# A third seven-product pair in the down projections, and the mixer's transposes' transfers issued from SyncE

## The chip, the cores and the metric

The kernel runs on one core of one Trainium2 chip. The time is device microseconds of one execution of the whole layer, from the first to the last instruction with what lies around them. The core's engines are TensorE (PE, with its weight loads as PEld), VectorE (DVE), ScalarE (ACT), GpSimd (POOL) and SyncE (SP); each runs its own list of instructions in order and waits on semaphores. DMA engines move data between HBM and the on-chip SBUF, on request of SP, POOL or ACT.

## The reference

One decoder layer in float32: 256 positions, model width 2048, inner width 5632. Cut to what matters:

```
def swiglu(h, w_gate, w_up, w_down):
    return (jax.nn.silu(h @ w_gate) * (h @ w_up)) @ w_down

x = x + 0.5 * swiglu(rms_norm(x, ffn1_norm), ffn1_w_gate, ffn1_w_up, ffn1_w_down)
h = rms_norm(x, mix_norm);  proj = h @ w_in
# q, k: per-head norm and rotary; dilated and differential attention -> o_dil, o_diff
y = sigmoid(g_dil) * (o_dil @ w_dil_branch) + sigmoid(g_diff) * (o_diff @ w_diff_branch)
x = x + y @ w_out
x = x + 0.5 * swiglu(rms_norm(x, ffn2_norm), ffn2_w_gate, ffn2_w_up, ffn2_w_down)
```

The middle part, between the two SwiGLU blocks, is called the mixer here.

## The kernel before

**Products.** Every float32 factor is split in two float32r parts, a high one (a rounded copy made by ACT) and a low one (the rest, a subtraction on DVE), and one product of blocks is three matmuls (`three`, L147 to L152): high x high, high x low, low x high. Each matmul takes 128 rows of the contraction, 128 positions and 512 columns of a weight. The activations stand in SBUF with the contraction on the partitions, 16 k tiles of 128 (20 or 24 for the down products), already split (`xh`, `xl`; `ah`, `al` for the down products).

**Weights.** They stream from HBM in pieces of 2 k tiles x 512 columns (512 KB), each into a tile `raw`, requested by SP. ACT and DVE split a piece into `w_hi` and `w_lo` (`parts`, L106, its instructions at L110 and L111; in `linear` L125 and L126). There are five pairs of split tiles, and four `raw` tiles, six inside the two SwiGLU blocks. A piece can be requested when a `raw` tile is free, that is when DVE has split what was in it, and it can be split when PE has used up an older split tile. So SP, ACT, DVE and PE form a chain of buffers that lets the splits run some pieces ahead of PE.

**Seven products for eight.** `two_chunks` (L176) computes two 512-column chunks at once. A pair of k tiles, u, is then a 2 x 2 block product (2 k tiles, 2 halves of the positions, 2 column chunks), which costs 8 block products, 24 matmuls. For the pairs named in `WINO` (gate and up) and `WINO_DOWN` (down), it takes seven block products, 21 matmuls, by sums of blocks (Winograd's form of Strassen's method). The sums of the x blocks are made once for all column chunks (`sums_of_x`, L154): per pair an addition, four small sums, a split, in a `raw` tile f that is held meanwhile. The sums of the weight blocks are made anew in each call: after the first split of the pair's two pieces, four subtractions on DVE overwrite the raw pieces (L217 to L220, L218 and after wait for each other), and then ACT and DVE split them a second time. So an ordinary pair needs two splits of 128x1024, and a seven-product pair three and a half and the four subtractions. After the last such pair ACT and DVE add up the partial results (L230 to L234), and at the end of a call DVE adds them to the others (L236).

**A SwiGLU block** (`ffn`, L361). Eleven chunks of 512 inner columns are done in two halves of 6 and 5 (`HALVES`). In a half, each chunk's gate and up columns are one call of `two_chunks` (the very first chunk is two calls of `linear`); DVE multiplies (L387), turns the result on 32x32 blocks (L279), and two DMAs through HBM finish the transpose (`turn_blocks`, L273, issued from POOL: `blocks<-turned`, then `moved<-blocks` once the first has landed). A deferred `split_blocks` then writes `ah`, `al`. At the end of a half the sums of x for the down products are made, and the down products follow: two calls of `two_chunks` in the first half, one and two `linear` in the second. So there are six such calls in the kernel's two blocks, and four "half starts", where the down products begin right behind the last gate and up chunk. On DVE the end of that chunk (L231 to L236, L387, L279) stands between the splits for the down products.

**The mixer** also uses `turn_blocks`, for the queries and keys (`qk_chunk`, L560), for y and for the residual. POOL runs its DMA requests and the powers for the norms (L246) in one list.

**Order.** The order on each engine is made when the kernel is built, by a scheduler that takes the program in the order written and moves instructions by its own estimate of when they can start.

Of the kernel before, what the change touches and what calls it, by code (L numbers as in the profile page):

```python
# [11 lines left out]
F32 = mybir.dt.float32  # L12
F32R = mybir.dt.float32r
I32 = mybir.dt.int32
AF = mybir.ActivationFunctionType
ALU = mybir.AluOpType
# [3 lines left out]
P = 128  # L20
# [14 lines left out]
WINO = (3, 5)  # L35
WINO_DOWN = (3, 6)
HALVES = (6, 5)
# [18 lines left out]
def hybrid_layer_kernel(ctx: ExitStack, tc: tile.TileContext, a: dict, out: bass.AP):  # L56
    nc = tc.nc
# [95 lines left out]

    def sums_of_x(pool, pairs, xh, xl, name):  # L154


        sx = {}
        for u in pairs:
            f = raw_tile()
            x, sm = f[:, 0].rearrange("p (k s) -> p k s", s=S), f[:, 1].rearrange("p (i m) -> p i m", m=P)  # L160
            nc.vector.tensor_tensor(x, xh[:, 2 * u:2 * u + 2].bitcast(F32), xl[:, 2 * u:2 * u + 2].bitcast(F32),
                                    op=ALU.add)
            a00, a01, a10, a11 = x[:, 0, :P], x[:, 1, :P], x[:, 0, P:], x[:, 1, P:]
            nc.vector.tensor_tensor(sm[:, 0], a10, a11, op=ALU.add)
            nc.vector.tensor_tensor(sm[:, 1], sm[:, 0], a00, op=ALU.subtract)
            nc.vector.tensor_tensor(sm[:, 2], a10, a00, op=ALU.subtract)
            nc.vector.tensor_tensor(sm[:, 3], a01, sm[:, 1], op=ALU.subtract)
            h, l = pool.tile([P, 4, P], F32R, name=f"{name}_h{u}"), pool.tile([P, 4, P], F32R, name=f"{name}_l{u}")
            nc.scalar.activation(h, sm, AF.Copy)
            nc.vector.tensor_tensor(l, sm, h.bitcast(F32), op=ALU.subtract)  # L170
            sx[u] = h, l
        return sx
# [3 lines left out]
    def two_chunks(cols, xh, xl, nk, sx, tmp):  # L176
# [15 lines left out]
        for u in range(nu):  # L192
# [14 lines left out]
            st, sp = u == first_sum, u == last_sum  # L207
            sm = lambda i: (sx[u][0][:, i], sx[u][1][:, i])
            part = lambda hl, k: (hl[0][:, k], hl[1][:, k])
# [39 lines left out]
    def split(hi, lo, src, gain=None):  # L249

        if gain is None:
            nc.scalar.activation(hi, src, AF.Copy)
            nc.vector.tensor_tensor(lo, src, hi.bitcast(F32), op=ALU.subtract)
        else:
            nc.scalar.activation(hi, src, AF.Copy, scale=gain)  # L255
            nc.vector.scalar_tensor_tensor(lo, src, gain, hi.bitcast(F32), op0=ALU.mult, op1=ALU.subtract)  # L256
# [15 lines left out]

    def turn_blocks(srcs, pool, x=None):  # L273

        r = pool.tile([P, 4, NT, 4, 32], F32, name="turned")
        for t in range(NT):
            nc.vector.transpose(r[:, :, t], srcs[t].rearrange("p (kt i q) -> p q kt i", i=32, q=4))  # L279
        d = dram.tile([4, P, NT * P], F32, name="blocks")  # L280
        nc.gpsimd.dma_start(d.rearrange("a (i q) x -> (a i) q x", q=4), r.rearrange("p q t kt j -> p q (t kt j)"))
        if x is None:
            x = pool.tile([P, 4, NT, 4, 32], F32, name="moved")
        nc.gpsimd.dma_start(x.rearrange("p a t kt j -> p a (t kt j)"), d.rearrange("a p x -> p a x"))
        return x
# [75 lines left out]
    def ffn(wg, wu, wd, norm, done, ahead=None):  # L361
        with tc.tile_pool(name="act", bufs=1) as apool, tc.tile_pool(name="actw", bufs=1) as aw, \
# [6 lines left out]
            j = 0  # L369
            for half, count in enumerate(HALVES):  # L370
                down = wd[j * CH:(j + count) * CH]
                for i in range(count):
                    if j == 0:
# [5 lines left out]
                        up = linear(wu, 0, xh, xl, KD)  # L379
                        sx = sums_of_x(sxp, WINO, xh, xl, "sx")  # L380
                    else:
# [4 lines left out]
                    for t in range(NT):  # L386
                        nc.vector.scalar_tensor_tensor(sg[t], up[t], rs[t], sg[t], op0=ALU.mult, op1=ALU.mult)  # L387
                    x = turn_blocks(sg, bp)
                    defer(BLOCK_WAIT, lambda x=x, i=i: split_blocks(x, ah, al, 4 * i))
# [479 lines left out]
```

## Time and profile before

| | |
|---|---|
| median of 3 runs | 2123.31 us (2119.55 to 2126.64) |
| the profiled execution | 2119.51 us, its span 2117.7 us |
| PE busy in the span | 2102.6 us, 99% |
| DVE / ACT / POOL busy | 1589.1 us (75%) / 1082.5 us (51%) / 100.2 us (5%) |
| granted TensorE clock | full speed in every slice |
| HBM traffic | 215 GB/s mean |

PE is busy nearly all the time, and the chain of work that ended last runs through PE for 94% of the span. So a time is saved where PE has fewer instructions, and lost where PE has to wait. The remaining idle time of PE stands in few places, and the view of waits lists them. A busy share of 75% on DVE is an average; in stretches DVE works without a gap.

### The profile page before, as it was taken

Reading aid. Unit: us, or ns where it says so; the run is one execution under the profiler, and the core shown is the slowest. Engines: PE = TensorE matmul, PEld = TensorE weight load, DVE = VectorE, ACT = ScalarE, POOL = GpSimd, SP = SyncE. Lnnn points to the kernel's source line nnn. Section 1 sums busy time; section 2 is a strip of 40 time slices with the busy share of each in tenths; the row PEclk is TensorE's granted clock in tenths of the full one; section 3 lists DMA queues with packets and bytes.
Section 4 is the critical chain, followed back from the end, with each engine's and each line's share of the span. In section 5 each row is a group of like instructions: output and inputs, shape, how many; then the busy total and the mean of one; then the engine's idle time right before and its main releaser. Section 6 shows DMA issues by size and latency. Waiting matters only on the chain.

```text
span 2117.7 us, 25700 instructions
## 1 busy us (share of the span) xinstructions
PE 2102.6 (99%) x9334; PEld 1736.9 (82%) x9334; DVE 1589.1 (75%) x2048; ACT 1082.5 (51%) x1335; POOL 100.2 (5%) x132
## 2 busy tenths in 40 slices
PE   9999999999999999999999999999999999999999
PEld 7888888888888888878888888888888888888887
DVE  6888987688898666677755556666898877888883
ACT  6555554455455545465555444554554544455542
POOL 1000000000000011011100000000000000000000
PEclk9999999999999999999999999999999999999999
DMA  8666665576668676766555667665676656567673
GB/s 282 218 216 210 224 236 188 186 242 227 215 209 275 224 232 196 237 190 216 192 188 159 207 223 250 228 224 179 227 241 214 210 207 218 196 218 233 207 251 125
DMA packets 224836, 456.29 MB, mean 215 GB/s; under 512 B 14098, under 2 KB 14660, under 8 KB 224452
## 3 DMA queue, kind: packets, MB, share of 16 engines
q1 hardware_dynamic: 212512, 411.09, 58.5%
q0 software_dynamic: 12096, 43.52, 6.4%
q8 instruction: 73, 1.20, 0.2%
q14 instruction: 55, 0.45, 0.1%
q10 hardware_dynamic: 100, 0.03, 0.0%
HBM read 428.89 MB, written 25.69 MB: 215 GB/s over the span
## 4 chain that ended last, share of the span: by engine, by line
PE 94%; DMA 2%; DVE 2%; ACT 1%; issue 1%; POOL 0%; ACTq 0%; POOLq 0%; DVEq 0%
PE mm L141 12%; PE mm L142 12%; PE mm L143 12%; PE mm L151 9%; PE mm L152 9%; PE mm L150 9%; PE tr L151 5%; PE tr L152 5%; PE tr L150 5%; PE s L150 5%; PE s L151 5%; PE s L152 5%; DMA q<-blocks 1%; DMA blocks<-turned 1%; DVE w_lo L126 1%
## 5 line engine op out<-in xcount | busy, mean ns | idle before, releaser
L110 ACT ACTIVATE w_hi<-raw 128x1024 fp32r<-128x1024 f32 (+1 forms) x560 | 553.0, 1016 | 540.8 <-DVE raw L220 183.7
L111 DVE TENSOR_TENSOR w_lo<-raw,w_hi 128x1024 fp32r<-128x1024 f32 (+1 forms) x560 | 639.4, 1170 | 163.1 <-ACT w_hi L110 161.0
L126 DVE TENSOR_TENSOR w_lo<-raw,w_hi 128x1024 fp32r<-128x1024 f32 (+1 forms) x313 | 378.9, 1218 | 259.5 <-ACT w_hi L125 256.6
L125 ACT ACTIVATE w_hi<-raw 128x1024 fp32r<-128x1024 f32 (+1 forms) x313 | 328.3, 1056 | 300.4 <-PE mm L143 250.0
L141 PE MATMUL mm<-w_hi,xh 128*128 128x512 f32 x864 | 339.2, 394 | 0.0
L142 PE MATMUL mm<-w_lo,xh 128*128 128x512 f32 x864 | 338.9, 393 | 0.0
L143 PE MATMUL mm<-w_hi,xl 128*128 128x512 f32 x864 | 336.7, 393 | 0.0
L151 PE MATMUL mm<-w_lo,xh 128*128 128x512 f32 x540 | 210.2, 389 | 0.0
L152 PE MATMUL mm<-w_hi,xl 128*128 128x512 f32 x540 | 210.1, 389 | 0.0
L150 PE MATMUL mm<-w_hi,xh 128*128 128x512 f32 x540 | 201.0, 389 | 0.0
L142 PEld LDWEIGHTS mm<-w_lo,xh 128*128 128x128 f32 x864 | 162.8, 188 | 33.5
L141 PEld LDWEIGHTS mm<-w_hi,xh 128*128 128x128 f32 x864 | 162.7, 188 | 33.6 <-ACT xh L255 0.2
L143 PEld LDWEIGHTS mm<-w_hi,xl 128*128 128x128 f32 x864 | 162.5, 188 | 33.6 <-DVE xl L256 0.2
L150 PEld LDWEIGHTS mm<-w_hi,xh 128*128 128x128 f32 x540 | 101.3, 188 | 21.1
L151 PEld LDWEIGHTS mm<-w_lo,xh 128*128 128x128 f32 x540 | 101.4, 188 | 21.0
L152 PEld LDWEIGHTS mm<-w_hi,xl 128*128 128x128 f32 x540 | 101.4, 188 | 21.0
L151 PE MATMUL tr<-w_lo,xh 128*128 128x512 f32 x280 | 108.9, 389 | 0.0
L150 PE MATMUL tr<-w_hi,xh 128*128 128x512 f32 x280 | 108.9, 389 | 0.0
L152 PE MATMUL tr<-w_hi,xl 128*128 128x512 f32 x280 | 108.9, 389 | 0.0
L151 PE MATMUL s<-w_lo,xh 128*128 128x512 f32 x260 | 101.1, 389 | 0.0
L150 PE MATMUL s<-w_hi,xh 128*128 128x512 f32 x260 | 101.1, 389 | 0.0
L152 PE MATMUL s<-w_hi,xl 128*128 128x512 f32 x260 | 101.1, 389 | 0.0
(280 smaller groups left out, 3240.3 us busy)
## 6 DMA issues: line engine op xcount, KB each, us to landing
raw<-in_w_in_dram SPq DMA_DIRECT2D x184, 512.0 KB, 4.1
raw<-in_ffn_w_up_dram SPq DMA_DIRECT2D x176, 512.0 KB, 4.9
raw<-in_ffn_w_down_dram SPq DMA_DIRECT2D x176, 512.0 KB, 5.4
raw<-in_ffn_w_gate_dram SPq DMA_DIRECT2D x175, 512.0 KB, 4.5
blocks<-turned POOLq DMA_DIRECT2D x41, 512.0 KB, 3.9
raw<-in_w_out_dram SPq DMA_DIRECT2D x32, 512.0 KB, 5.1
moved<-blocks POOLq DMA_DIRECT2D x31, 512.0 KB, 4.3
raw<-in_w_diff_branch_dram SPq DMA_DIRECT2D x16, 512.0 KB, 5.3
```

The source lines that it names most:

```text
L110: last_hi = nc.scalar.activation(hi[:, :n], src, AF.Copy)
L111: last_lo = nc.vector.tensor_tensor(lo[:, :n], src, hi[:, :n].bitcast(F32), op=ALU.subtract)
L125: last_hi = nc.scalar.activation(hi[:, ks], raw[:, ks], AF.Copy)
L126: last_lo = nc.vector.tensor_tensor(lo[:, ks], raw[:, ks], hi[:, ks].bitcast(F32), op=ALU.subtract)
L141: nc.tensor.matmul(ps[t], xh[:, k, sl], hi[:, kk], start=k == 0, stop=False)
L142: nc.tensor.matmul(ps[t], xh[:, k, sl], lo[:, kk], start=False, stop=False)
L143: nc.tensor.matmul(ps[t], xl[:, k, sl], hi[:, kk], start=False, stop=k == nk - 1)
L150: nc.tensor.matmul(ps, h, wh, start=start, stop=False)
L151: nc.tensor.matmul(ps, h, wl, start=False, stop=False)
L152: nc.tensor.matmul(ps, l, wh, start=False, stop=stop)
```

## The change

`WINO_DOWN` gets a third pair: (2, 5, 7) instead of (3, 6). To have room for the third pair's sums, the fourth sum of x for gate and up (S4) no longer has a tile of its own: it is written over the block of `xh`, `xl` that the seven products no longer use (`over`), as a split of its own. `turn_blocks` issues its two DMAs from SyncE unless told otherwise; inside `ffn` it is told GpSimd as before. So 38 of the 82 transfers of that kind, those of the queries, keys, y and the residuals, move into the list in which SP requests the weights.

```
-WINO_DOWN = (3, 6)
+WINO_DOWN = (2, 5, 7)
...
-    def sums_of_x(pool, pairs, xh, xl, name):
+    def sums_of_x(pool, pairs, xh, xl, name, over=()):
...
-            h, l = pool.tile([P, 4, P], F32R, name=f"{name}_h{u}"), pool.tile([P, 4, P], F32R, name=f"{name}_l{u}")
-            nc.scalar.activation(h, sm, AF.Copy)
-            nc.vector.tensor_tensor(l, sm, h.bitcast(F32), op=ALU.subtract)
-            sx[u] = h, l
+            n = 3 if u in over else 4
+            h, l = pool.tile([P, n, P], F32R, name=f"{name}_h{i}"), pool.tile([P, n, P], F32R, name=f"{name}_l{i}")
+            split(h, l, sm[:, :n])
+            sx[u] = [(h[:, i], l[:, i]) for i in range(n)]
+            if u in over:
+                sx[u].append((xh[:, 2 * u, P:], xl[:, 2 * u, P:]))
+                split(*sx[u][3], sm[:, 3])
...
-    def turn_blocks(srcs, pool, x=None):
+    def turn_blocks(srcs, pool, x=None, queue=None):
+        queue = queue or nc.sync
...
-        nc.gpsimd.dma_start(d.rearrange("a (i q) x -> (a i) q x", q=4), r.rearrange("p q t kt j -> p q (t kt j)"))
+        queue.dma_start(d.rearrange("a (i q) x -> (a i) q x", q=4), r.rearrange("p q t kt j -> p q (t kt j)"))
...
-        nc.gpsimd.dma_start(x.rearrange("p a t kt j -> p a (t kt j)"), d.rearrange("a p x -> p a x"))
+        queue.dma_start(x.rearrange("p a t kt j -> p a (t kt j)"), d.rearrange("a p x -> p a x"))
...
-                        sx = sums_of_x(sxp, WINO, xh, xl, "sx")
+                        sx = sums_of_x(sxp, WINO, xh, xl, "sx", WINO[-2:])
...
-                    x = turn_blocks(sg, bp)
+                    x = turn_blocks(sg, bp, queue=nc.gpsimd)
```

In the program as built, PE has 9240 matmuls instead of 9258, DVE 64 more instructions and ACT 20 more.

Two places in the new order. The first is DVE's list at the half start of the second half of the first SwiGLU block, before the change. `raw_5126` and `raw_5128` are the pieces of the down products' pair 2, an ordinary pair here, `raw_5162` and `raw_5164` those of pair 3, their first seven-product pair; `turned` is the end of the last gate and up chunk.

```order
L111 TENSOR_TENSOR w_lo_5131<-raw_5126,w_hi_5130 128x1024
L387 SCALAR_TENSOR_TENSOR e_4689<-x_4691,rr1_376,e_4689 128x512
L387 SCALAR_TENSOR_TENSOR u2_4690<-y_4692,rr1_382,u2_4690 128x512
L111 TENSOR_TENSOR w_lo_5147<-raw_5128,w_hi_5146 128x1024
L279 STREAM_TRANSPOSE turned_5016<-e_4689 128x4x128
L279 STREAM_TRANSPOSE turned_5016<-u2_4690 128x4x128
L111 TENSOR_TENSOR w_lo_5167<-raw_5162,w_hi_5166 128x1024
L111 TENSOR_TENSOR w_lo_5177<-raw_5164,w_hi_5176 128x512
L217 TENSOR_TENSOR raw_5162<-raw_5164,raw_5162 128x512
L218 TENSOR_TENSOR raw_5164<-raw_5164 128x512
L219 TENSOR_TENSOR raw_5164<-raw_5164,raw_5162 128x512
L220 TENSOR_TENSOR raw_5162<-raw_5162,raw_5164 128x512
```

And the same place of DVE's list after the change, where `raw_5132` and `raw_5134` are pair 1, and `raw_5168` and `raw_5170` pair 2, now the first seven-product pair; `sd_l2` is the third pair's split sum of x.

```order
L257 TENSOR_TENSOR sd_l2_5082<-raw_5075,sd_h2_5081 128x512
L111 TENSOR_TENSOR w_lo_5153<-raw_5134,w_hi_5152 128x1024
L392 SCALAR_TENSOR_TENSOR e_4721<-x_4723,rr1_376,e_4721 128x512
L392 SCALAR_TENSOR_TENSOR u2_4722<-y_4724,rr1_382,u2_4722 128x512
L111 TENSOR_TENSOR w_lo_5173<-raw_5168,w_hi_5172 128x1024
L111 TENSOR_TENSOR w_lo_5183<-raw_5170,w_hi_5182 128x512
L284 STREAM_TRANSPOSE turned_5048<-e_4721 128x4x128
L284 STREAM_TRANSPOSE turned_5048<-u2_4722 128x4x128
L221 TENSOR_TENSOR raw_5168<-raw_5170,raw_5168 128x512
L222 TENSOR_TENSOR raw_5170<-raw_5170 128x512
L223 TENSOR_TENSOR raw_5170<-raw_5170,raw_5168 128x512
L224 TENSOR_TENSOR raw_5168<-raw_5168,raw_5170 128x512
```

The end of the chunk stands ahead of the first seven-product pair's subtractions in both; two splits fewer and one sum of x more stand before them in the new list, and what they serve is one pair earlier in PE's list.

The second place is POOL's list in the mixer, before the change: the powers for the norms stand between the two DMAs of a key chunk.

```order
L246 TENSOR_TENSOR rr4_8083<-rv4_8081,mhalf_91 128x4
L246 TENSOR_TENSOR rr4_8102<-rv4_8100,mhalf_91 128x4
L246 TENSOR_TENSOR rr1_8190<-rv1_8188,mhalf_91 128x1
L281 DMA blocks_8117<-turned_8114 128x1024
L284 DMA dk_7030<-blocks_8117 128x4x256
L246 TENSOR_TENSOR rr1_8200<-rv1_8198,mhalf_91 128x1
```

After the change the DMAs stand in SP's list, a weight's piece between the two; here another key chunk.

```order
L123 DMA raw_7798<-in_w_in_dram 128x2x512
L286 DMA blocks_7525<-turned_7522 128x1024
L123 DMA raw_7836<-in_w_in_dram 128x2x512
L289 DMA dk_7081<-blocks_7525 128x4x256
L123 DMA raw_7854<-in_w_in_dram 128x2x512
```

What waited for such a DMA on POOL no longer stands behind it; the requests for weights now do.

## Rows read from the trace of the kernel before

**Rows 1.** The page: engines' busy time, then the chain's shares by engine.
```profile
PE 2102.6 (99%) x9334; PEld 1736.9 (82%) x9334; DVE 1589.1 (75%) x2048; ACT 1082.5 (51%) x1335; POOL 100.2 (5%) x132
...
PE 94%; DMA 2%; DVE 2%; ACT 1%; issue 1%; POOL 0%; ACTq 0%; POOLq 0%; DVEq 0%
```

**Rows 2.** PE's waits in the mixer: us in total, times, longest.
```profile
PE s L675 <- ACT on L680: 1.6, 1, 1.6
PE tr L688 <- ACT on L680: 1.4, 2, 0.9
PE s L722 <- DMA dk<-blocks: 1.2, 1, 1.2
```

**Rows 3.** PE's timeline, a steady stretch (start us, us, engine, line, what).
```profile
310.12 0.39 PE L151 MATMUL mm<-w_lo,ah 128*128 128x512 f32 x1
...
317.37 0.39 PE L152 MATMUL mm<-w_hi,al 128*128 128x512 f32 x1
```

**Rows 4.** DVE's timeline, half start in the first block's second half.
```profile
591.86 2.36 DVE L111 TENSOR_TENSOR w_lo<-raw,w_hi 128x1024 fp32r<-128x1024 f32 x2 [1.21 <-ACT w_hi L110]
594.14 0.69 DVE L161 TENSOR_TENSOR raw<-ah,al 128x512 f32<-128x512 f32 x1
...
599.15 0.29 DVE L164 TENSOR_TENSOR raw<-raw 128x128 f32<-128x128 f32 x1
599.35 0.29 DVE L166 TENSOR_TENSOR raw<-raw 128x128 f32<-128x128 f32 x1
...
606.87 1.22 DVE L111 TENSOR_TENSOR w_lo<-raw,w_hi 128x1024 fp32r<-128x1024 f32 x1 [1.82 <-ACT w_hi L110]
...
610.41 0.68 DVE L170 TENSOR_TENSOR sd_l<-raw,sd_h 128x512 fp32r<-128x512 f32 x1
611.01 1.22 DVE L111 TENSOR_TENSOR w_lo<-raw,w_hi 128x1024 fp32r<-128x1024 f32 x1
...
623.38 0.69 DVE L220 TENSOR_TENSOR raw<-raw 128x512 f32<-128x512 f32 x1
```

**Rows 5.** PE's timeline: the first product of twice-split weights at each half start.
```profile
285.17 0.39 PE L150 MATMUL tr<-w_hi,sd_h 128*128 128x512 f32 x1
...
625.29 0.50 PE L150 MATMUL mm<-w_hi,sd_h 128*128 128x512 f32 x1 [0.17 <-ACT w_hi L110]
...
1685.02 0.50 PE L150 MATMUL mm<-w_hi,sd_h 128*128 128x512 f32 x1 [0.36 <-ACT w_hi L110]
...
2024.30 0.39 PE L150 MATMUL tr<-w_hi,sd_h 128*128 128x512 f32 x1
```

**Rows 6.** DVE's timeline: the last subtraction before each of the other three, and gaps.
```profile
265.23 1.22 DVE L111 TENSOR_TENSOR w_lo<-raw,w_hi 128x1024 fp32r<-128x1024 f32 x1 [1.42 <-ACT w_hi L110]
...
282.51 0.69 DVE L220 TENSOR_TENSOR raw<-raw 128x512 f32<-128x512 f32 x1
...
1683.11 0.69 DVE L220 TENSOR_TENSOR raw<-raw 128x512 f32<-128x512 f32 x1
...
2004.59 1.23 DVE L111 TENSOR_TENSOR w_lo<-raw,w_hi 128x1024 fp32r<-128x1024 f32 x1 [1.64 <-ACT w_hi L110]
...
2021.10 0.69 DVE L220 TENSOR_TENSOR raw<-raw 128x512 f32<-128x512 f32 x1
```

**Rows 7.** ACT's waits, 584 to 626 us; then in the mixer, 840 to 1100.
```profile
ACT w_hi L110 <- DMA raw<-in_ffn_w_down_dram: 8.1, 5, 2.5
...
ACT w_hi L125 <- PE mm L143: 49.0, 35, 3.0
```

**Rows 8.** POOL's timeline in the mixer: a key chunk's second DMA and a power.
```profile
990.89 0.77 POOL L284 DMA_DIRECT2D dk<-blocks  x1 [4.66 <-DMA blocks<-turned]
991.67 0.57 POOL L246 TENSOR_TENSOR rr<-rv,mhalf 128x1 f32<-128x1 f32 x1
```

**Rows 9.** DMA issues of the page: KB each, median us from issue to landing.
```profile
blocks<-turned POOLq DMA_DIRECT2D x41, 512.0 KB, 3.9
...
x_mid<-xs SPq DMA_DIRECT2D x4, 512.0 KB, 5.7
```

More of the change, by code (lines that the diff above doesn't have):

```diff
@@ L152, in three @@
         nc.tensor.matmul(ps, l, wh, start=False, stop=stop)
-    def sums_of_x(pool, pairs, xh, xl, name):
+    def sums_of_x(pool, pairs, xh, xl, name, over=()):
         sx = {}
-        for u in pairs:
+        for i, u in enumerate(pairs):
             f = raw_tile()
@@ L207, in two_chunks @@
             st, sp = u == first_sum, u == last_sum
-            sm = lambda i: (sx[u][0][:, i], sx[u][1][:, i])
+            sm = lambda i: sx[u][i]
             part = lambda hl, k: (hl[0][:, k], hl[1][:, k])
```

## The prediction

> **What bounds the kernel now.** I read the page first: PE is busy for 99% of the span, and 94% of the chain that ended last runs through PE [rows 1]. The reader is to see that only two things move the time: matmuls that are no longer there, and waits of PE that come or go. Then I read PE's waits: in the mixer they are 1.6, 1.4 and 1.2 us [rows 2], 4.2 us in all, and that is all that the mixer could ever give back. Then I read DVE, which prepares the low parts of the weights, not by its share of the whole span but at the half starts, where the down products begin [rows 4 to 6]. There DVE works almost without a gap from the end of one seven-product pair to the next one's subtractions, and PE takes the twice-split weights as they become ready.
>
> **Products taken away.** Six calls get one seven-product pair more, each with 3 matmuls fewer: 18 matmuls, which is also the difference of the two lists. One matmul costs PE its distance to the next: from 310.12 to 317.37 us there are 32 of them, so 0.2266 us each [rows 3]. 18 x 0.2266 = 4.1 us saved, on the path that sets the end, if PE is fed.
>
> **The half starts.** This is the term that decides. In the first block's second half, DVE ends the last subtraction at 623.38 + 0.69 = 624.07 [rows 4], and PE's first product of the transformed weights starts at 625.29, after a wait [rows 5]: 1.22 us later, the time of ACT's copy. So PE stands right behind DVE there. By the same 1.22 us the weights were ready at 284.42, 1685.02 and 2023.01 in the other three starts [rows 6], and PE took them at 285.17, 1685.02 and 2024.30 [rows 5]: 0.75, 0 and 1.29 us of slack.
>
> The new first pair is pair 2 instead of pair 3. So PE comes to it one ordinary pair earlier, 24 matmuls x 0.2266 = 5.44 us. DVE doesn't come earlier by as much. Its list up to the subtractions loses the two splits of that ordinary pair, each 2.28 / 2 = 1.14 us (the row of two at 591.86 ends where the next begins, at 594.14), and gains the third sum of x: an addition and a subtraction at 0.60 us (610.41 to 611.01) and four small ones at 0.20 us (599.15 to 599.35), 2.0 us [rows 4]. That is 2.28 - 2.0 = 0.28 us earlier. What could be moved behind the subtractions, the end of the gate and up chunk with its two block transposes, stays ahead of them in the new list too. So PE is late by 5.44 - 0.28 = 5.16 us, less the slack: 4.4, 5.2, 5.2 and 3.9 us, 18.6 us in all. PE gives none of it back, since behind each start it runs at its own pace.
>
> From below: DVE is not quite full in these stretches. Its gaps are 1.82 us [rows 4], 1.42 and 1.64 us [rows 6], some 1.6 us a start. They come from ACT waiting for pieces of the down weights [rows 7], and the third sum could be computed in them. If it filled them all, 4 x 1.6 = 6.5 us fall away and 12.1 us stay. From above: each sum of x holds one of the six raw tiles, here from 594.14 to 611.09 us [rows 4]. A third one leaves three tiles for weights, and if each start's weights come one piece later for it, that is 12 matmuls, 2.7 us a start, 10.9 us more: 29.5 us. I take the middle of the two nearer ends, 15.3 us: DVE's gaps are measured and the sums are spread over them in the new list, but the missing tile works against it.
>
> Behind the first pair nothing changes much: from pair 2 to 5 there are two ordinary pairs, as there were from 3 to 6. From 5 to 7 there is one. From one pair's transformed weights to the next's, DVE then has the second splits of pair 5 and those of pair 6 (four, 4.56 us), one and a half of pair 7 (1.71), four subtractions at 0.69 (2.76) [rows 4] and the 1.22 us of ACT's copy: 10.25 us. PE has 12 + 24 + 9 matmuls in between, 10.2 us. I count nothing for it; a lateness here would be a few tenths a start. The later call of the first half begins with no gate and up chunk in front of it, and I count nothing there either.
>
> **S4 over x.** Two more instructions on ACT and DVE per pair, 8 in all, each small (0.29 us on DVE, as the small sums [rows 4]), where DVE is far from full. The split now waits until PE has read the block for the up products, and the splits of the next pieces stand behind it. They run ahead of PE, which hides it; without that cover a block loses up to one piece, 2.7 us. I take 0.
>
> **The transfers on SyncE.** 38 DMAs leave POOL's list and stand in SP's. What they were in the way of on POOL: one power for the norms starts at 991.67, the moment the key chunk's second DMA is issued [rows 8], and PE waits for what follows from it; that is at most 0.5 us of the 1.4 us at L688 [rows 2]. What they are in the way of on SP: the request of the next weights, for as long as the first transfer takes to land, 3.9 us in the median [rows 9]. ACT mostly waits for PE to free a split tile in the mixer, 35 times [rows 7], so the splits are ahead and a request late by 3.9 us should stay hidden; without that cover it would cost a part of 3.9 us at each of 19 transposes. How fast the moved transfers run on SP's queue can't be seen in before. The only row of that size from SBUF to HBM on SP's queue, `x_mid`, took 5.7 us against 3.9 on POOL's [rows 9], 1.8 us more; through both transfers that makes 3.6 us more in front of the one place where PE waits for them, 1.2 us now [rows 2]. So from below the mixer gains 4.2 us (all its waits gone), and from above it loses 3.6 us there and about as much again where ACT waits for queries. I take a gain of 0.5 us.
>
> A rule speaks on each side here. The Trainium skill, "DMA: Bandwidth & Descriptors", section "Latency and other measured facts", gives a first byte after about 0.6 us from SyncE and about 1 us from GpSimd. By that the chain of two transfers is 0.8 us shorter and the mixer gains 1.3 us instead of 0.5. The same page, section "Queues, rings and completion order", says that a DMA engine takes turns between queues but works through one queue's ring in order, so that a transfer moved into the weights' queue starts behind the weights requested before it. The row of `x_mid` agrees with the second, and by it the mixer loses.
>
> **The sum.** -4.1 + 15.3 + 0 - 0.5 = +10.7 us. On the profiled execution's 2119.5 us that is 2130.2 us; that execution lay 3.8 us under the median of the runs, so in their terms 2134 us, 0.5% slower.
>
> **The rivals.**
>
> *The starts stay covered; not slower.* Place: the four starts. If DVE comes to the first seven-product pair on average less than (4.1 + 0.5 + 6.4) / 4 = 2.7 us late, the result is no longer slower by 0.3% (6.4 us). For it: DVE's gaps, and two of the starts had slack. Against it: filling all gaps still leaves 12.1 us, so a part of DVE's list would have to be shorter than its rows add up to. With 1.1 us a start: 2123.3 + 4.4 - 4.6 = 2123 us. Chance 0.19.
>
> *The saving comes whole and the mixer gives up its waits.* No lateness, -4.1 - 4.2: 2115 us, faster by 0.4%. For it: the waits of rows 2 are real. Against: two unlikely things at once. Chance 0.05.
>
> *The mixer pays.* SP's list makes weights and transposes late in the mixer: 7 us more on top of the forecast, 2141 us. For it: the row of `x_mid`, and that SP's list now waits for DVE, for transfers and for free tiles in turn. Against: the splits are ahead of PE. The second of the two rules above would bring this about. Chance 0.10.
>
> **How the numbers follow.** The forecast has 0.66, the rivals 0.19, 0.05 and 0.10. About 0.3% is what a measurement of this kernel can tell from no change. The ends of the forecast's own sum are 12.1 - 4.1 - 4.2 = +3.8 and 18.6 - 4.1 + 3.6 = +18 us, and one missing piece at half of the starts makes it +23. So 2122 to 2146 us, which also takes in most of the first rival. Faster 0.05, same 0.21, slower 0.74.
>
> **What would show it.** PE with 18 matmuls less. At each half start, waits of PE on ACT's or DVE's split in front of the first product of pair 2's transformed weights, 2 to 5 us each, where there were 0 to 0.4; DVE without a gap in front of them. The four waits in the mixer changed by no more than a few us in sum. The forecast is wrong if PE's waits at the four starts stay under 11 us in sum, or if PE waits for weights in the mixer.

## The result, and the profile after

The changed kernel takes 2141.5 us (median of 6 runs, 2137.0 to 2147.5), where the kernel before has 2126.8 us over the runs beside it: the ratio is 1.009, with a 95% interval of 1.0071 to 1.0109. So it is slower by 0.7 to 1.1%; 2134 us were forecast, in a range of 2122 to 2146. Of the runs further on, one of e1 (3563.7 us) and one of e4 (12006.8 us) are far off all others of their kernels and stand in no median and no ratio. The profiled execution has a span of 2138.6 us. First the page: engines' busy time, then the chain's shares, as in [rows 1].

```profile
PE 2108.9 (99%) x9316; PEld 1739.5 (81%) x9316; DVE 1624.5 (76%) x2112; ACT 1095.9 (51%) x1355; POOL 79.0 (4%) x94
...
PE 89%; DVE 5%; DMA 3%; issue 2%; ACT 1%; POOL 0%; ACTq 0%; DVEq 0%; POOLq 0%
```

PE has 18 matmuls less than in [rows 1] and is still busy 6.3 us longer, and outside its busy time it stands idle for 29.7 us instead of 15.1. DVE and DMA have gained shares of the chain: PE now waits. Where, its timeline tells: the first product of twice-split weights at each half start and the waits just ahead of it, as in [rows 5].

```profile
282.88 0.50 PE L150 MATMUL tr<-w_hi,sd_h 128*128 128x512 f32 x1 [2.92 <-ACT w_hi L110]
...
618.86 0.50 PE L150 MATMUL mm<-w_hi,ah 128*128 128x512 f32 x1 [0.51 <-ACT w_hi L110]
...
626.60 0.80 PE L150 MATMUL mm<-w_hi,sd_h 128*128 128x512 f32 x1 [3.13 <-ACT w_hi L110]
...
1694.53 0.80 PE L150 MATMUL mm<-w_hi,sd_h 128*128 128x512 f32 x1 [3.21 <-ACT w_hi L110]
...
2035.03 0.50 PE L151 MATMUL mm<-w_lo,sd_h 128*128 128x512 f32 x1 [0.76 <-DVE w_lo L111]
2038.25 0.50 PE L150 MATMUL tr<-w_hi,sd_h 128*128 128x512 f32 x1 [2.49 <-ACT w_hi L110]
```

With the small waits beside them (0.2 to 0.5 us) these are 3.1, 3.6, 4.1 and 4.0 us, 14.9 us in all; before they were 1.4 us. The end of each is what ended it in the forecast, the second split behind the subtractions. In the mixer the three waits of [rows 2] have become one:

```profile
PE s L727 <- DMA dk<-blocks: 4.2, 1, 4.2
```

The granted clock was at full speed everywhere before. Now it is not. The windows of PE around the second half start (PE, PEld, DVE, ACT and POOL busy with instructions, then the granted clock, the DMA share and GB/s):

```profile
622.00:627.00 5.00, 1.87 (x8) 1.29 (x7) 3.69 (x6) 1.51 (x2) 1.18 (x2) 0.88 0.26 105
627.00:631.00 4.00, 4.00 (x10) 2.88 (x10) 4.00 (x4) 3.79 (x5) 0.12 (x1) 0.50 0.70 209
631.00:635.00 4.00, 4.00 (x15) 3.18 (x15) 3.80 (x6) 2.70 (x4) 0.00 (x0) 0.80 0.81 259
635.00:640.00 5.00, 5.00 (x23) 4.14 (x23) 4.47 (x6) 0.91 (x2) 0.00 (x0) 1.00 0.96 361
```

Behind the wait of 3.13 us the granted clock is 0.50, that is 1.2 instead of 2.4 GHz, until 632.6 us (0.80 as the mean of 631 to 635 us is 1.6 us at 0.50). PE's timeline shows the pitch there, 0.43 us instead of the 0.2266 of [rows 3]:

```profile
628.56 0.63 PE L151 MATMUL mm<-w_lo,sd_h 128*128 128x512 f32 x1
628.99 0.63 PE L152 MATMUL mm<-w_hi,sd_l 128*128 128x512 f32 x1
629.42 0.63 PE L151 MATMUL s<-w_lo,ah 128*128 128x512 f32 x1
```

A stretch at 0.50 stands behind each of the other three half starts too and behind the wait on `dk`, and, but for the last microsecond of the span, nowhere else. PE's busy time times what is missing to a clock of 1.00, summed over windows of 5 us, is 8.6 us: 7.1 us behind the half starts, 1.5 us behind `dk`.

How the weights come to the second half start can be read on three engines. The first fence is a line of DVE before the change that [rows 4] lacks, the last subtraction of the gate and up chunk. The second is the timeline of DVE (to be read beside [rows 4]), ACT and SP after the change, the third a wait of SP in it.

```profile
589.96 0.69 DVE L220 TENSOR_TENSOR raw<-raw 128x512 f32<-128x512 f32 x1
```

```profile
591.73 0.69 DVE L224 TENSOR_TENSOR raw<-raw 128x512 f32<-128x512 f32 x1
...
614.77 0.68 DVE L257 TENSOR_TENSOR sd_l<-raw,sd_h 128x512 fp32r<-128x512 f32 x1
616.00 1.23 DVE L111 TENSOR_TENSOR w_lo<-raw,w_hi 128x1024 fp32r<-128x1024 f32 x1 [0.55 <-ACT w_hi L110]
...
624.68 0.69 DVE L224 TENSOR_TENSOR raw<-raw 128x512 f32<-128x512 f32 x1
...
614.91 1.06 ACT L110 ACTIVATE w_hi<-raw 128x1024 fp32r<-128x1024 f32 x1 [2.92 <-DMA raw<-in_ffn_w_down_dram]
...
615.48 0.37 SPq L200 DMA_DIRECT2D raw<-in_ffn_w_down_dram  x1
```

```profile
SPq L200 <- DVE sd_l L257: 2.0, 1, 2.0
```

From the last subtraction of the gate and up chunk (591.73 + 0.69) to 624.68 + 0.69 DVE needs 32.95 us, where before (589.96 to 623.38) it was 33.42 us: it comes 0.47 us earlier, 0.28 was forecast. PE's first product of the twice-split weights follows the end of the last subtraction by 1.23 us (625.37 to 626.60), as before: PE stands right behind DVE. DVE is nearly full: it waits for ACT three times, 0.60, 0.55 and 0.28 us, 1.43 us in all (1.82 before). ACT waits for pieces of the weights there, and SP can't request one until the third sum's tile is free at 614.77 + 0.68 = 615.45; that piece is the last one in front of the subtractions. So at this start late pieces can account for at most 1.4 of the 3.6 us of waits; the rest is the length of DVE's list.

### The profile page after: what moved, and what is told of

Its sections match the earlier page's. It is cut to its first block, busy times and chain, and to the rows that moved or that the text cites. A ratio compares the mean times of both kernels' runs of the same rounds, so it can differ in the third digit from the quotient of the medians.

```text
span 2138.6 us, 25737 instructions
## 1 busy us (share of the span) xinstructions
PE 2108.9 (99%) x9316; PEld 1739.5 (81%) x9316; DVE 1624.5 (76%) x2112; ACT 1095.9 (51%) x1355; POOL 79.0 (4%) x94
## 4 chain that ended last, share of the span: by engine, by line
PE 89%; DVE 5%; DMA 3%; issue 2%; ACT 1%; POOL 0%; ACTq 0%; DVEq 0%; POOLq 0%
PE mm L141 13%; PE mm L142 13%; PE mm L143 13%; PE mm L150 8%; PE mm L151 8%; PE mm L152 8%; PE tr L152 4%; PE tr L151 4%; PE tr L150 4%; PE s L150 4%; PE s L151 4%; PE s L152 4%; DVE w_lo L111 2%; DMA raw<-in_ffn_w_down_dram 1%; ACT w_hi L110 1%
## 5 line engine op out<-in xcount | busy, mean ns | idle before, releaser
L110 ACT ACTIVATE w_hi<-raw 128x1024 fp32r<-128x1024 f32 (+1 forms) x572 | 562.8, 1013 | 560.5 <-DVE raw L224 215.7
L125 ACT ACTIVATE w_hi<-raw 128x1024 fp32r<-128x1024 f32 (+1 forms) x313 | 328.7, 1056 | 309.5 <-PE mm L143 256.1
L142 PE MATMUL mm<-w_lo,xh 128*128 128x512 f32 x864 | 339.9, 394 | 0.0
L141 PE MATMUL mm<-w_hi,xh 128*128 128x512 f32 x864 | 339.3, 394 | 0.0
L143 PE MATMUL mm<-w_hi,xl 128*128 128x512 f32 x864 | 337.5, 393 | 0.0
L151 PE MATMUL mm<-w_lo,xh 128*128 128x512 f32 x560 | 218.0, 389 | 0.0
L152 PE MATMUL mm<-w_hi,xl 128*128 128x512 f32 x560 | 217.9, 389 | 0.0
L150 PE MATMUL mm<-w_hi,xh 128*128 128x512 f32 x560 | 208.8, 389 | 0.0
L143 PEld LDWEIGHTS mm<-w_hi,xl 128*128 128x128 f32 x864 | 163.1, 189 | 33.9 <-DVE xl L260 0.2
L152 PEld LDWEIGHTS mm<-w_hi,xl 128*128 128x128 f32 x560 | 105.1, 188 | 21.8
L150 PE MATMUL tr<-w_hi,xh 128*128 128x512 f32 x300 | 116.7, 389 | 0.0
L151 PE MATMUL tr<-w_lo,xh 128*128 128x512 f32 x300 | 116.7, 389 | 0.0
L152 PE MATMUL tr<-w_hi,xl 128*128 128x512 f32 x300 | 116.7, 389 | 0.0
```

The lines of the kernel that those rows point to most:

```text
L110: last_hi = nc.scalar.activation(hi[:, :n], src, AF.Copy)
L125: last_hi = nc.scalar.activation(hi[:, ks], raw[:, ks], AF.Copy)
L141: nc.tensor.matmul(ps[t], xh[:, k, sl], hi[:, kk], start=k == 0, stop=False)
L142: nc.tensor.matmul(ps[t], xh[:, k, sl], lo[:, kk], start=False, stop=False)
L143: nc.tensor.matmul(ps[t], xl[:, k, sl], hi[:, kk], start=False, stop=k == nk - 1)
L150: nc.tensor.matmul(ps, h, wh, start=start, stop=False)
```

## The experiments

Twelve further runs were made. The ratios are to the kernel before, of runs on the same chip, with 95% intervals; kernels are compared with each other by their ratios or their spans, since their chips differ.

**e1, e2, e5: the queue, S4 and the third pair apart.** e1 is the changed kernel with

```
-WINO_DOWN = (2, 5, 7)
+WINO_DOWN = (3, 6)
```

> The changed kernel with the old pairs (3, 6) of the down products; S4 over x and the transfers on SyncE stay. Theory (the earlier first pair at the half starts costs it all): PE's waits at the four half starts fall from 14.9 us to about 1.4, the granted clock stays at 1.00 behind them, and the time is that of the kernel before within 3 us; what is left of the change is the mixer, where one wait on `dk` of about 4 us stands in place of four, with some 1.7 us of lower clock behind it. Rival (S4 over x and the moved transfers cost a good part): 5 us or more above the kernel before.

e2 is the changed kernel with `queue = queue or nc.gpsimd`.

> The changed kernel with all block transposes' transfers back on GpSimd's queue; the third pair and S4 over x stay. Theory: the half starts are as in the changed kernel (about 15 us of waits, clock down behind each), the wait on `dk` in the mixer goes from 4.2 back to 1.2 us and the waits on `on` (3.0 us in sum) come back; total within 2 us of the changed kernel, perhaps 1.7 us less since the clock doesn't fall behind a wait of 1.2 us. Rival (SyncE's queue is what makes weights late): 8 us or more below the changed kernel.

e5 is the kernel before with the new `turn_blocks` (SyncE in the mixer, GpSimd inside `ffn`).

> The kernel before with the mixer's block transposes' transfers issued from SyncE, nothing else changed. e1, with this and S4 over x, ran 11 us below the kernel before (0.9948), though its profiled execution lies only 5.3 us below that of before. Theory (the queue brings it): 0.993 to 0.997, and PE's four waits in the mixer (4.2 us) are gone. Rival (S4 over x brings it): within 0.2% of the kernel before, with the waits in the mixer still there.

| | median, us | ratio | span, us |
|---|---|---|---|
| e1: SyncE, S4 | 2114.2 | 0.9948 (0.9936 to 0.9960) | 2112.4 |
| e5: SyncE alone | 2116.2 | 0.9949 (0.9932 to 0.9966) | 2114.7 |
| e2: third pair, S4 | 2149.8 | 1.0112 (1.0094 to 1.0129) | 2148.2 |

Of e1 I expected the time of the kernel before; it came out 11 us faster. e5 was made to find out why and has the same gain, as its theory said. e1 and e5 agree within 0.2%, so S4 has no cost that these runs can tell, and the queue brings the 11 us. In e2 the half starts are as its theory has them (15.0 us of waits), but on the time both its expectations failed: it is no faster than the changed kernel, and its wait on `dk` is 8.0 us instead of 1.2. All waits of PE for weights in e1 are these (us in total, times, longest); for `on` and `dk` there is none:

```profile
PE tr L150 <- ACT w_hi L110: 0.7, 2, 0.4
PE s L150 <- ACT w_hi L110: 0.4, 2, 0.2
```

From e1's span to the changed kernel's, only the pairs differ: 26.2 us. It is made up of -4.1 (products), +14.7 (half starts, 14.9 against 0.2), +4.2 (`dk`), +8.6 (clock), +0.6 (waits at the first pair of gate and up in the second block, 1.3 against 0.7) and 2.2 that stay open; the first product behind a wait takes 0.50 to 0.80 us instead of 0.39, which is a part of them. So the third pair and its place cost about 26 us, and the queue gives 11 us back with two pairs; how much of it the changed kernel keeps, the runs don't tell well (1.0112 to 1.0090, about 5 us, with intervals that overlap; by the spans 9.6 us).

**e8: the kernel before once more.** Nothing is changed; a second profile was wanted, since the first one is of its fastest run.

> The kernel before once more, for its profile: its profiled execution (2119.5 us) is the fastest of all its runs, which have a median of 2126.6 us and mostly a mean clock of 0.999. Theory: a usual execution loses 5 to 8 us at a longer wait on `dk` in the mixer, with a lower clock behind it. Rival: it loses them in many places.

It took 2130.4 us, span 2128.6. PE's waits in the mixer:

```profile
PE s L722 <- DMA dk<-blocks: 3.8, 1, 3.8
PE tr L688 <- ACT on L680: 2.3, 2, 1.4
PE s L675 <- ACT on L680: 1.9, 1, 1.9
PE tr L663 <- DVE pr L655: 0.8, 1, 0.8
```

That is 8.8 us, where [rows 2] gave 4.2, and behind `dk` the clock falls to 0.50 for 6 us (2.8 us lost by the sum used above), where the first profile has full speed. The theory held for the longest wait; the others grew too. This run lies 3 us above the median of the 23 runs beside it (2127.3 us, 2123.0 to 2133.8), and the first profile lay below all of them: the two are a slower and a faster execution of one kernel. What is late can be read from the DMA issues of that stretch (KB each, us to landing), of this run at 1061 to 1075 us and then of e5 at 1053 to 1064 us, the same key chunk:

```profile
blocks<-turned POOLq DMA_DIRECT2D x1, 512.0 KB, 6.4
dk<-blocks POOLq DMA_DIRECT2D x1, 512.0 KB, 5.4
```

```profile
blocks<-turned SPq DMA_DIRECT2D x1, 512.0 KB, 3.5
dk<-blocks SPq DMA_DIRECT2D x1, 512.0 KB, 4.1
```

The two transfers take 7.6 us from SyncE and 11.8 us from GpSimd. In that stretch the weights beside them are late too (6.2 us in e8, 4.7 in e5, in the median), so this one chain doesn't show that the queue is the reason. The whole mixer (640 to 1470 us) shows more; its first transfers in the first profile of the kernel before, then in e5:

```profile
blocks<-turned POOLq DMA_DIRECT2D x20, 512.0 KB, 4.9
```

```profile
blocks<-turned SPq DMA_DIRECT2D x19, 512.0 KB, 4.2
```

They take 4.9, 5.1 and 5.0 us in the median from GpSimd (before, e8, e2) and 4.2, 4.1 and 4.3 us from SyncE (e5, e1, changed); the second transfers take 5.2 to 7.0 and 3.9 to 5.3 us, while the weights of `w_in` take 3.8 to 4.3 us in all six. So the moved transfers themselves land sooner from SyncE. The Trainium skill, "SBUF — State Buffer", section "SBUF: two separate sides", gives a reason why a transfer from GpSimd can be slow: its descriptors are written by GpSimd, which VectorE shuts out while it runs an operation in a two-port mode, and it advises SyncE's or ScalarE's queue. The durations agree with the advice; that this is the cause no run here shows, and GpSimd's own instructions for the two transfers take 0.60 and 0.77 us in the fast and the slow profile alike.

**e3, e4, e6: the place of the first pair, and the third sum.** Each is the changed kernel with other pairs: e3 `(2, 6)`, e4 `(4, 6, 8)`, e6 `(3, 5, 7)`. In e4 the second half takes pair 8's sum from rows that its last block hasn't filled yet: it leaves out that wait, its output isn't the layer's, and its times say little of the second and fourth start.

> Pairs (2, 6) of the down products: the first pair is as early as in the changed kernel, but there is no third pair and no third sum of x. Theory (what costs is that PE comes to the first pair one ordinary pair earlier): DVE comes earlier by two splits, 2.28 us, PE by 4.1 to 5.4, so waits of 1.5 to 3 us at each start, 6 to 12 us in all, and a lower granted clock behind them; 8 to 16 us above the kernel before. Rival (the third sum, which takes a raw tile, is what makes the weights late): waits under 3 us in all, and a time within 4 us of the kernel before.

> Pairs (4, 6, 8) of the down products: three pairs as in the changed kernel, but the first one ordinary pair later than in the kernel before. Theory (only the place of the first pair costs): DVE has 2.28 + 2.0 us more to do than in the kernel before until then, PE 5.4 us more, so no waits at the half starts; the whole saving of 4.1 us stays, less the mixer's 1 to 2 us: 2 to 5 us below the kernel before, 16 to 20 below the changed one. Rival (a third pair leaves too few raw tiles, so weights come late wherever it stands): waits of 5 us or more at the half starts, and a time above the kernel before.

> Pairs (3, 5, 7) of the down products: three pairs, the first where the kernel before had it; S4 over x and SyncE as in the changed kernel. Theory (the costs of the third pair are the early first pair and the clock that falls behind its waits): DVE is 2.0 us later at each half start for the third sum, less the slack and its gaps (0 to 1.3 and about 0.4), so waits of 0 to 1.6 us each, 4 us in all, no or little loss of clock; with the 4.1 us saved that is level with e1 (2112 to 2120 us), unless the wait on `dk` of about 4 us is there again, then 2118 to 2125. Rival (a third sum alone keeps the raw tiles from the weights): waits over 2 us at each start, clock down, over 2128 us.

| | median, us | ratio | waits at the half starts, us |
|---|---|---|---|
| e3: (2, 6) | 2131.5 | 1.0021 (1.0012 to 1.0029) | 9.3 |
| e6: (3, 5, 7) | 2131.2 | 1.0023 (1.0011 to 1.0035) | 6.0, and 2.9 at pair 5 |
| changed: (2, 5, 7) | 2141.5 | 1.0090 (1.0071 to 1.0109) | 14.9 |
| e4: (4, 6, 8) | 2124.0 | 0.9989 (0.9979 to 0.9998) | 3.6 |

The early pair alone brings 9.3 us of waits. A third pair with the first one left in its place brings as much, 6.0 us at the starts and 2.9 at pair 5, which comes one pair sooner than pair 6 did. Together they bring 14.9 us, less than the sum. e3 lies 5 us above the kernel before and not 8 to 16, since the queue's 11 us, not known when that was written, are in its time. PE's timeline of e3 at the first three half starts:

```profile
282.33 0.50 PE L150 MATMUL tr<-w_hi,sd_h 128*128 128x512 f32 x1 [1.54 <-ACT w_hi L110]
...
624.80 0.50 PE L150 MATMUL mm<-w_hi,sd_h 128*128 128x512 f32 x1 [2.95 <-ACT w_hi L110]
...
1684.18 0.50 PE L150 MATMUL mm<-w_hi,sd_h 128*128 128x512 f32 x1 [2.77 <-ACT w_hi L110]
```

The forecast's terms for e3 are 5.44 - 2.28 = 3.16 us late, less the slack of each start: 2.4, 3.2, 3.2 and 1.9. Measured, with the small waits: 1.8, 3.2, 3.0 and 1.4. For e6 they are 2.0 us late less the slack, 1.3, 2.0, 2.0 and 0.7; measured 2.4, 1.7, 0.2 and 1.7. So e3 follows DVE's list within 0.7 us a start, e6 only in sum. e6's rival (over 2 us at each start, over 2128 us) is right on the time and wrong on the waits. e4 waits 3.5 us at `dk` again and loses 2.4 us of clock behind it. Its span is 11.8 us longer than e1's, so without these two it would still lie above e1, with 18 matmuls less. So no place of a third pair that was tried is as good as two pairs.

**e7: work in place of the wait.** The changed kernel with 14 useless products at each half start, in front of the first product of the twice-split weights (`fill` is 14 in the first call of a half):

```
             three(c01, sm(3), part(b, 0), False, False)
+            for _ in range(fill if st else 0):
+                nc.tensor.matmul(p5, xh[:, 0, :P], b[0][:, 0], start=True, stop=True)
```

> The changed kernel, and at each of the four half starts 14 products that nothing uses (into the bank that the first product of the transformed weights clears), in front of that product: 14 x 0.2266 = 3.2 us of work in place of the wait. Theory (TensorE's granted clock falls because PE stands still, and costs 8.5 us behind the four starts): the waits shrink to under 1 us each, the weights come no earlier, the clock stays at 1.00 behind the starts, and the time falls by 6 to 9 us against the changed kernel though 56 matmuls are added. Rival (the clock falls for another reason, or the slow matmuls cost nothing because DVE is late anyway): time level with the changed kernel or above it.

It took 2131.3 us, ratio 1.0020 (1.0009 to 1.0031), against 1.0090: 56 matmuls more, and 0.7% less; the span is 9.2 us shorter. Its windows at the second half start, to be laid beside those of the changed kernel:

```profile
622.00:627.00 5.00, 4.75 (x20) 3.30 (x18) 3.69 (x6) 1.82 (x2) 1.30 (x2) 1.00 0.26 105
627.00:631.00 4.00, 3.79 (x18) 3.12 (x18) 4.00 (x5) 4.00 (x6) 0.00 (x0) 1.00 0.72 217
631.00:635.00 4.00, 4.00 (x19) 3.34 (x18) 3.73 (x5) 2.24 (x4) 0.00 (x0) 1.00 0.92 272
```

The waits at the four starts are 2.7 us, 12.2 less, and the added products take 56 x 0.2266 = 12.7 us in their place. The weights hardly come earlier (626.29 against 626.60 us at the second start), and the clock stays at 1.00 behind all four. So the lower clock is a price of its own of PE's standing still, and it was 7 us of the changed kernel's time. The rest of the gain is shorter waits, on `dk` (2.5 instead of 4.2 us) and at the first pair of gate and up in the second block (0.2 instead of 1.3).

**e9, e10: the sums of x on GpSimd.** The changed kernel, and e6, with `eng.tensor_tensor` for the five instructions of a sum, `eng=nc.gpsimd` for the down products.

> The changed kernel with the sums of x for the down products (the addition, the three subtractions and the sum of each pair, five instructions) computed on GpSimd instead of VectorE. Theory (at the half starts PE waits for VectorE, whose list is too long): VectorE loses 3 x 2.0 = 6.0 us in front of each half start, more than the 2.9 to 4.0 us that PE waits there, so the waits fall under 1 us each and the clock stays up; 20 to 25 us below the changed kernel if the wait on `dk` goes too, 15 to 20 if it stays. Rival (the raw tiles that the sums hold are the limit): GpSimd is slower at them and holds the tiles longer, so the waits stay as they are or grow, and the time is that of the changed kernel or more.

> Pairs (3, 5, 7) as in e6, with the sums of x for the down products on GpSimd. Theory: e6's 9 us of waits at the half starts fall under 2 us in all, and the time comes to 2112 to 2120 us, up to 4 us under e5 (0.993 to 0.997 of the kernel before), more if the wait on `dk` is still there. Rival (raw tiles): waits as in e6 or more, 2130 us or above.

e9 took 2141.1 us, 1.0064 (1.0047 to 1.0081), e10 2135.3 us, 1.0034 (1.0022 to 1.0046). My theory failed here: the waits at the starts of e9 are 15.8 us, as long as in the changed kernel, and those of e10 12.5 us. An addition is slower on GpSimd (ns, smallest, median and largest):

```profile
L163 POOL TENSOR_TENSOR raw<-ah,al x12: 2201/2273/2278, 253.3 to 2012.0; 128x512 f32<-128x512 f32 x12
```

2.27 us instead of 0.60, with the `raw` tile held all the while, and ACT waits up to 5.4 us for a down piece, 4.2 us in the changed kernel. So the rival's outcome came. But its reason can't be told from e9, because DVE wasn't relieved either. The five instructions of a sum were 1.4 us there by [rows 4], 4.2 us a start (the 6.0 of the expectation counts the split's subtraction too, which stays on DVE). And DVE's own instructions take longer while GpSimd adds. Six splits in a row at the second start:

```profile
595.93 9.64 DVE L111 TENSOR_TENSOR w_lo<-raw,w_hi 128x1024 fp32r<-128x1024 f32 x6 [1.21 <-ACT w_hi L110]
```

That is 1.6 us each, where two in a row took 2.36 us in [rows 4]. From the last subtraction of the gate and up chunk to the last one of the first down pair DVE needs 32.91 us in e9 (from 594.03 to 626.94) and 32.95 in the changed kernel.

**e12: one raw tile less.** e1 with `FFN_RAW = 1`, five `raw` tiles, and DVE's list as it was.

> e1 (two pairs, S4 over x, SyncE) with five raw tiles in the feed-forward blocks instead of six; no third sum and VectorE's list as in e1. Theory (a third sum costs as much by the raw tile that it holds as by VectorE's time): the down pieces are requested later and PE waits 1.5 to 3 us at each half start, 6 to 12 us in all, with clock lost behind the longer ones: 8 to 20 us above e1. Rival (VectorE's time alone sets the start, the tiles have room): under 2 us of waits in all at the starts, within 4 us of e1.

It took 2129.9 us, 1.0037 (1.0024 to 1.0049), 19 us above e1 by the ratios and by the spans. PE waits 10 us at the half starts, as in the first and the third:

```profile
289.74 0.50 PE L150 MATMUL tr<-w_hi,sd_h 128*128 128x512 f32 x1 [2.91 <-ACT w_hi L110]
...
1686.71 0.50 PE L150 MATMUL tr<-w_hi,ah 128*128 128x512 f32 x1 [2.36 <-ACT w_hi L110]
```

So the tile alone, with no instruction added, brings waits of the size that e6 has. But here the tile is gone all through the two blocks, while a sum holds one for some 17 us at each start. How much of a third sum is DVE's time and how much the tile, DVE's timelines tell. The table has the stretches used above (last subtraction of gate and up to last subtraction of the first down pair), summed over the four starts, and the idle time of DVE in them (gaps of 0.15 us and more, without the first, ACT's copy):

| | stretches, us | idle in them, us |
|---|---|---|
| before | 134.0 | 7.2 |
| e1: (3, 6) | 133.0 | 6.1 |
| e3: (2, 6) | 122.1 | 5.1 |
| e6: (3, 5, 7) | 144.6 | 9.2 |
| changed: (2, 5, 7) | 133.3 | 7.7 |
| e12: a tile less | 141.9 | 14.4 |

e12's 8.8 us over e1 are idle time of DVE, which waits for pieces. e6's 11.6 us over e1 are 8.5 us of work, 2.1 us a start as the forecast has it, and 3.1 us of idle time. So a third sum costs mostly DVE's time, and about a quarter of its cost is waiting for pieces that come late; that these are late for its tile is likely by e12, not shown.

**e11: the third sum behind the half start.** Pairs (3, 6) as before, and a third pair in the half's last block, `third = 2 * (count - 1)`, whose sum is made inside the first call:

```
         for u in range(nu):
+            if late and u == late[0] - 3:
+                sx.update(late[1]())
```

> The first two pairs as in the kernel before (3, 6), and a third pair that lies in the half's last block (pair 10 or 8), whose sum of x is computed inside the first call, behind the half start; S4 over x and SyncE as in the changed kernel. Theory (a third pair costs only where it is in front of a half start): PE's waits up to the first product of the transformed weights stay under 1 us a start as in e1, the third sum lies beside products and the 18 matmuls are saved: 2 to 6 us under e1 and e5, about 2110 to 2114 us, 0.992 to 0.994 of the kernel before; 4 to 6 us more if the wait on `dk` in the mixer is there, as in all kernels with three pairs so far. Rival (VectorE has no room for a third sum and a third pair anywhere): waits of 1 to 3 us in front of the second or third pair of each call, over 2122 us.

It took 2127.7 us, 1.0033 (1.0020 to 1.0047). The first products of the twice-split weights come without a wait over 0.4 us, as the theory has it, but waits now stand further on in the same call:

```profile
304.40 0.50 PE L150 MATMUL tr<-w_hi,sd_h 128*128 128x512 f32 x1 [1.90 <-ACT w_hi L110]
...
639.60 0.80 PE L150 MATMUL tr<-w_hi,ah 128*128 128x512 f32 x1 [4.45 <-ACT w_hi L110]
```

With a third of 2.5 us and the small ones beside them they are 9.3 us. The rival is right in this: in that place, too, a third sum and pair bring PE to wait in the first call of a half. Other places in the call were not tried.

**The wait on `dk`.** No run was made for this one alone; the lists and traces of the others tell it. All four kernels with two pairs and SyncE (e1, e3, e5, e12) have no such wait, and all seven with three pairs and SyncE have one of 2.0 to 4.4 us. In SP's list the three-pair kernels all have two requests for weights between the two transfers of the second differential query chunk, the others one. SP's timeline of e1, then of the changed kernel:

```profile
1027.00 0.34 SPq L286 DMA_DIRECT2D blocks<-turned  x1
1029.40 0.37 SPq L123 DMA_DIRECT2D raw<-in_w_in_dram  x1
1032.78 0.37 SPq L289 DMA_DIRECT2D q<-blocks  x1
```

```profile
1035.06 0.34 SPq L286 DMA_DIRECT2D blocks<-turned  x1
1037.45 3.09 SPq L123 DMA_DIRECT2D raw<-in_w_in_dram  x2
1042.60 0.37 SPq L289 DMA_DIRECT2D q<-blocks  x1
```

From the first transfer to the second it is 5.8 us there and 7.5 us here: the second request for weights has to wait for a free tile, and the query's transfer behind it. ACT's copy of that query stands ahead of the next key chunk's first instruction, so the key chunk, `dk`, comes later by as much and more. One more difference stands in SP's lists: the first two pieces of the second block's gate weights are requested before this query chunk in every kernel with three pairs (at 1032.70 us in the changed kernel), and some 150 us later in those with two (at 1175.94 us in e1). So the scheduler orders the mixer otherwise when the down products have a third pair; why, and which of the differences makes the wait, was not tried.

## Why the prediction was right, and where it was not

- **Products, -4.1 us.** Right in the count, 9316 matmuls instead of 9334; by [rows 3] that is 4.1 us, and no run shows it alone.
- **Half starts, +15.3 us.** Right in place and mechanism: 14.9 us, 13.5 more than before, 3.1 to 4.1 at each start; the forecast's condition, over 11 us, is met. At all four starts PE's first product of the twice-split weights follows the end of DVE's last subtraction by 1.2 us, so PE stands behind DVE's list, and e3 and e6 show the two parts of the list, the earlier pair and the third sum, each by itself. That the size is so close is in part luck. The forecast took 3.3 us off for gaps of DVE that the third sum would fill; in sum DVE's idle time there is 7.2 us before and 7.7 after, so nothing was filled, and the sign "DVE without a gap" did not come. In its place PE came to the pair less early than reckoned: without its waits, and counted from DVE's last subtraction of gate and up, it would come 5.3, 3.9, 3.1 and 4.4 us earlier than before at the four starts, where 5.44 was taken for each. That is 5.1 us less in sum, for which the forecast had no term; its cause was not looked for. The missing tile, which the forecast took as something that may add to DVE's time, can have added at most the 3.1 of 11.6 us that are idle time in e6.
- **Behind the first pair, 0.** Right for the changed kernel: no wait at pairs 5 and 7. A lateness came in e6, from pair 3 to pair 5, 0.7 us a start.
- **S4, 0.** Right within 0.2%, by e1 against e5.
- **Mixer, -0.5 us.** This step failed, though the two profiled executions have the same 4.2 us of waits. Its best case, "all its waits gone", -4.2 us, was read from one execution that was the fastest of the kernel before; a slower one waits 8.8 us and loses 2.8 us of clock, and e5, where all these waits are gone, gains 11 us. Of the waits it laid only 0.5 us to POOL's list; with the transfers on SyncE all of them go with two pairs, and all but the one on `dk` with three. That one, 4.2 us instead of 1.2, stands behind requests for weights in SP's list, as the forecast feared in kind. What it feared of SyncE's queue, transfers slower than from GpSimd, didn't come: it set `x_mid`, 5.7 us, against 3.9, but the 3.9 of [rows 9] is the median of all 41 transfers, over half of them in the SwiGLU blocks; in the mixer alone it is 4.9, and 4.2 from SyncE. The time of the third rival, 2141 us, is the measured one, by chance: it came with a mixer that pays 7 us more, and e2 against the changed kernel and e5 against the kernel before show that SyncE makes the mixer shorter. Of the two rules of the Trainium skill weighed there ("DMA: Bandwidth & Descriptors", sections "Latency and other measured facts" and "Queues, rings and completion order"), the first has the right sign and too small a size (0.8 us for a chain of two transfers, 7.6 against 11.8 us in the chain shown), and what the second would bring is not seen in the transfers' times.
- **The clock had no term.** 7.1 us behind the half starts and 1.5 us behind `dk`. The forecast priced a wait at its length; in the changed kernel they cost nearly half as much again.

The last two have opposite signs. Against the slower execution e8 (2128.6 us) the changed kernel's span is 10.0 us longer: -4.1 (products), +13.0 (half starts, against 1.9), -4.6 (mixer, 4.2 against 8.8), +5.8 (clock, 8.6 against 2.8), +0.9 (the second block's first pair), and -1.0 of rest. The forecast's +10.7 is close to that by two errors that cancel. By the medians (2126.8 and 2141.5 us) the change costs 14.7 us.

The kernel to keep is e5 or e1, 0.5% faster than the kernel before and 1.4% faster than the changed one (0.9949 / 1.0090 = 0.986).

## What to carry to other kernels

A wait that ends on a DMA is not known from one execution: where a sum rests on it, take a second profile, and ask whether the first is a usual run or the fastest. A buffer that new work borrows has a price beside the engine's time (e12): who requests into it, and when would that request have gone out? Moving work to an idle engine frees the busy one only if the two don't slow each other (e9). And where PE hardly ever waits, a wait of a few microseconds can cost more than its length, as a lower clock behind it has to be paid too; cheap useless products showed that here in one run.

## What the hardware showed beyond that

Not the length of a wait alone decides whether the clock falls. Behind 2.95 us (e3, 624.80) and 2.91 us (e12, 289.74) it stayed at 1.00, behind 2.77 us (e3, 1684.18) it fell. The windows of e11 show the shortest wait with a lower clock behind it, 1.45 us at 1482.86:

```profile
1480.00:1485.00 5.00, 3.34 (x13) 2.06 (x12) 3.79 (x5) 3.25 (x4) 0.00 (x0) 0.96 0.00 0
1485.00:1490.00 5.00, 5.00 (x17) 3.97 (x17) 4.96 (x7) 2.12 (x3) 0.00 (x0) 0.70 0.85 268
```

And those of e3 show the two waits of nearly one length, side by side:

```profile
624.00:630.00 6.00, 4.99 (x21) 3.84 (x22) 5.22 (x5) 5.49 (x6) 0.76 (x1) 1.00 0.54 165
...
1684.00:1690.00 6.00, 5.60 (x16) 4.17 (x17) 5.83 (x6) 5.77 (x8) 0.75 (x1) 0.72 0.61 181
```

What tells the two apart stays open. The other surprise is the spread of the transfers from GpSimd: in the first profile of the kernel before their chain to `dk` let PE wait 1.2 us, in the second 3.8, in e2, which has three pairs, 8.0, and in the four kernels with two pairs and SyncE not at all. And GpSimd's additions slow VectorE's splits beside them: six in a row took 1.6 us each in e9.
